# FFN's second product: inner tiles 4 to 15 in two blocks of seven block products instead of eight

## The chip, the core and the metric

The kernel is one program on one core of a Trainium2 chip. The metric is the device time of one execution, in microseconds. TensorE (PE) multiplies; VectorE (DVE) and ScalarE (ACT) prepare operands and take results out of PSUM; GpSimd (POOL) and SyncE (SP) issue DMAs.

## The reference, cut to what matters

One transformer layer on 512 tokens of width 1024, float32 throughout. The change lies in its last third, the feed-forward network:

```python
def _swiglu(h, w_in, w_out):
    g, u = jnp.split(h @ w_in, 2, axis=-1)
    return (jax.nn.silu(g) * u) @ w_out

x = x + g2 * _swiglu(_modulate(x, norm_ffn[l], sh2, sc2), w_ffn_in[l], w_ffn_out[l])
...
return _rmsnorm(x, norm_final)
```

The inner width is 2816, that is 22 tiles of 128. `g2` holds one gate per output channel.

## The kernel before, in words

**Three matmuls for one.** Every float32 operand is held as a high part (a rounding to `fp32r`) and a low part (what the rounding left). ACT makes the high part (`nc.scalar.copy`) and DVE subtracts it from the value to get the low part. `mm3` multiplies high by high, high by low and low by high: lines L187, L188 and L189, three matmuls for each 128-row slice of the inner dimension. `mm3_low_last` (L194, L195, L197) is the same with all matmuls of the weights' low parts at the end.

**Layout.** Channels lie on partitions and tokens on columns. The input of the FFN, `hp`, is held as four quarters (two halves of the channels by two halves of the 512 tokens, `T` = 512, `TC` = 256): `B11`, `B21`, `B22` and so on.

**FFN in.** For each of the 22 inner tiles there is a gate tile and an up tile. Tiles 0 to 2 are multiplied plainly. Tiles 3 to 21 go through `front` and `back`, called a *pair* here: the gate and up weights of tile j as the two rows of a 2 by 2 block matrix, the halves of the input channels as its columns, so that seven block products replace eight (Winograd's form of Strassen's scheme). A pair needs the sums S1 to S4 of weight quarters and the sums N1, N2, T3, T4 of input quarters. The input's sums were made once. The weights' sums and splits are made for each pair by `prepare`:

- loads: the gate tile into `wr` (3 buffers), the up tile into `ur` (2 buffers), both issued by SP;
- `A11`: high part on ACT, low part on DVE (`direct`, L1025 and L1027);
- S1 and S2 on DVE (L1042, L1043), split 1024 wide into `gh`/`gl`; S3 and S4 (L1048, L1049) into `wh`/`wl`;
- `A12` and `A22`: high part on ACT (L1025), its negative of the raw weight's rounding on ACT (L1029), and then a DMA issued by POOL that adds the raw weight from DRAM to it (L1030, accumulating DMA), so that DVE has nothing to do for them.

A product is 4 slices of 3 matmuls, 128x128 weights by 256 columns. I name the products in the order in which they run: `front` has f1 (A11 by B11), f2 (S1 by N1), f3 (S2 by N2), f4 (A12 by B21), `back` has b1 (S3 by T3), b2 (S4 by B22), b3 (A22 by T4). The loop in `strassen` staggers them: while pair j runs its front, pair j-1 runs its back, in the order f1 f2 b1 f3 b2 f4 b3. Between them stand short steps that read and write PSUM: ACT copies (L1068, L1072), DVE additions (L1075, L1086), the gate function on ACT (L1079, L1089), the two products gate times up on DVE (L1090, L1093, the latter after b3), and the split of the finished tile into `act` (L176, L177).

**FFN out.** When a block of inner tiles is done, `ffn_out` multiplies it plainly: for each of the 8 output tiles, 3 matmuls of 512 columns for each inner tile of the block, weights split by `wload` (L157 on ACT, L158 on DVE, two buffers each of `wh`, `wl`), and DVE adds g2 times the result to the residual `x1` in SBUF (L1251). Blocks are tiles 0 to 7, 8 to 14 and 15 to 21. The last block runs in halves of the tokens, with the final norm behind it.

**Order.** In this part the order on each engine is set by a scheduler with costs of its own; PE, ACT and DVE then run their lists strictly in order. DMAs wait in the lists of SP and POOL, in order too.

## Time and profile before

| | |
|---|---|
| median of the runs (lowest, highest) | 885.57 us (885.19, 886.25) |
| time of the profiled execution | 886.11 us |
| its span in the profile | 884.3 us |
| PE busy, share of the span | 874.4 us, 99% |
| DVE, ACT, POOL busy | 614.7, 436.7, 66.7 us |
| matmuls | 5920 recorded (5579 rows in PE's list, repeats merged) |
| granted TensorE clock, mean | 0.998 |

Times in rows of the profile count from the start of the span. A row of a timeline has the start, the duration, the engine, the line and the tiles written and read; in brackets stands the idle time of the engine before it and who ended it. Matmuls and most other instructions overlap with the next of their engine, so what one costs in a row of many is the distance of two starts, not the duration. In a table of groups, the last columns are busy time, mean duration and idle time before.

### The profile page before, as it was taken

How to read it: one execution, taken by the hardware profiler on the slowest of the kernel's cores; microseconds unless marked ns; L12 is line 12 of the kernel's file. 1: busy time of each engine (PE TensorE's matmuls, PEld its weight loads, DVE VectorE, ACT ScalarE, POOL GpSimd, SP SyncE). 2: the span in 40 equal slices, each digit the busy share in tenths (PEclk: the TensorE clock that was granted, in tenths of full speed). 3: DMA queues.
4: the chain of work that ended last, by engine and by line, in shares of the span. 5: the costliest groups of instructions: out<-in, count | busy, mean ns of one | idle time of the engine just before them, and what ended most of it. 6: DMA issues, size and time to landing. Idle time of an engine off the chain costs nothing.

```text
span 884.3 us, 15057 instructions
## 1 busy us (share of the span) xinstructions
PE 874.4 (99%) x5920; PEld 797.7 (90%) x5920; DVE 614.7 (70%) x1187; ACT 436.7 (49%) x823; POOL 66.7 (8%) x93
## 2 busy tenths in 40 slices
PE   9999999999999999999999999999999999999997
PEld 7689798899888998889988899999889998899996
DVE  4678677877876787767886767795366753867644
ACT  4464354455344453444455446673255741666542
POOL 0000010020000100000000000120011100111000
PEclk9999999999999999999999999999999999999999
DMA  9863021436252542434454830384366643755502
GB/s 349 324 196 113 25 72 57 164 113 180 72 187 88 170 141 84 155 109 135 142 149 125 294 111 1 104 221 107 95 176 147 145 119 87 206 142 125 144 1 96
DMA packets 41446, 120.88 MB, mean 137 GB/s; under 512 B 4480, under 2 KB 8864, under 8 KB 40352
## 3 DMA queue, kind: packets, MB, share of 16 engines
q1 hardware_dynamic: 35904, 109.96, 38.2%
q0 software_dynamic: 5472, 9.96, 6.8%
q8 instruction: 46, 0.75, 0.3%
q14 instruction: 24, 0.20, 0.1%
HBM read 116.22 MB, written 3.69 MB: 136 GB/s over the span
## 4 chain that ended last, share of the span: by engine, by line
PE 96%; DVE 1%; ACT 1%; DMA 1%; issue 0%; DVEq 0%; SPq 0%; ACTq 0%
PE ps L187 14%; PE ps L189 13%; PE ps L188 13%; PE ps L197 8%; PE ps L195 8%; PE ps L194 8%; PE pat L347 3%; PE ps L578 3%; PE ps L579 3%; PE ps L580 3%; PE pat L187 2%; PE pat L189 2%; PE pat L188 2%; PE pat L792 2%; PE pat L793 2%; PE pat L794 2%
## 5 line engine op out<-in xcount | busy, mean ns | idle before, releaser
L157 ACT CAST wh<-wr 128x1024 fp32r<-128x1024 f32 (+3 forms) x78 | 78.9, 1011 | 102.7 <-PE ps L188 45.6
L158 DVE TENSOR_TENSOR wl<-wr,wh 128x1024 fp32r<-128x1024 f32 (+3 forms) x78 | 92.6, 1188 | 35.9 <-ACT wh L157 23.8
L194 PE MATMUL ps<-a,wh 128*128 128x512 f32 x272 | 106.5, 392 | 0.0
L195 PE MATMUL ps<-a,wh 128*128 128x512 f32 x272 | 106.3, 391 | 0.0
L187 PE MATMUL ps<-act,wh 128*128 128x512 f32 (+1 forms) x199 | 69.2, 348 | 0.0
L188 PE MATMUL ps<-act,wh 128*128 128x512 f32 (+1 forms) x199 | 69.0, 347 | 0.0
L189 PE MATMUL ps<-act,wl 128*128 128x512 f32 (+1 forms) x199 | 69.0, 347 | 0.0
L197 PE MATMUL ps<-a,wl 128*128 128x512 f32 x272 | 68.0, 390 | 0.0
L195 PEld LDWEIGHTS ps<-a,wh 128*128 128x128 f32 x272 | 51.1, 188 | 10.2
L194 PEld LDWEIGHTS ps<-a,wh 128*128 128x128 f32 x272 | 51.1, 188 | 10.2
L197 PEld LDWEIGHTS ps<-a,wl 128*128 128x128 f32 x272 | 50.8, 188 | 10.5
L1030 POOL DMA_DIRECT2D ol<-in_wffi x38 | 33.4, 897 | 254.7 <-ACT ol L1029 124.4
L187 PE MATMUL ps<-hp,gh 128*128 128x256 f32 x176 | 49.9, 284 | 0.4 <-ACT gh L176 0.4
L189 PE MATMUL ps<-hp,ol 128*128 128x256 f32 x176 | 48.8, 277 | 0.5 <-DVE ol L1027 0.5
L188 PE MATMUL ps<-hp,gh 128*128 128x256 f32 x176 | 49.0, 278 | 0.0
L1251 DVE SCALAR_TENSOR_TENSOR x<-ps,lb,x 128x512 f32<-128x512 f32 (+1 forms) x32 | 19.6, 616 | 42.1 <-PE ps L189 42.1
L189 PE MATMUL ps<-hp,gl 128*128 128x256 f32 x176 | 48.9, 278 | 0.0
L187 PE MATMUL ps<-hp,oh 128*128 128x256 f32 x176 | 48.8, 277 | 0.0
L188 PE MATMUL ps<-hp,oh 128*128 128x256 f32 x176 | 48.7, 277 | 0.0
L537 DVE SCALAR_TENSOR_TENSOR pb<-pb,crow_s 128x1024 f32<-128x1024 f32 x32 | 38.9, 1233 | 10.1 <-DMA pb<-in_wada_b 10.1
L187 PEld LDWEIGHTS ps<-act,wh 128*128 128x128 f32 x199 | 37.5, 188 | 4.8
L188 PEld LDWEIGHTS ps<-act,wh 128*128 128x128 f32 x199 | 37.5, 188 | 4.8
(365 smaller groups left out, 2726.4 us busy)
## 6 DMA issues: line engine op xcount, KB each, us to landing
wr<-in_w SPq DMA_DIRECT2D x42, 512.0 KB, 3.5
pb<-in_wada_b SPq DMA_DIRECT2D x32, 512.0 KB, 4.2
wr<-in_wffi SPq DMA_DIRECT2D x25, 512.0 KB, 4.3
ur<-in_wffi SPq DMA_DIRECT2D x19, 512.0 KB, 4.0
ol<-in_wffi POOLq DMA_DIRECT2D x38, 256.0 KB, 4.9
ada<-in_wada_a SPq DMA_DIRECT2D x8, 1024.0 KB, 9.8
wr<-in_wffo SPq DMA_DIRECT2D x16, 448.0 KB, 3.6
wr<-in_wout SPq DMA_DIRECT2D x8, 512.0 KB, 3.5
```

The costliest lines, as they stand in the source:

```text
L157: nc.scalar.copy(wh, raw[:, :n])
L158: V.tensor_sub(wl, raw[:, :n], wh.bitcast(F32))
L187: nc.tensor.matmul(dst, wh, ah, start=first and i == 0, stop=False, skip_group_check=on)
L188: nc.tensor.matmul(dst, wh, al, start=False, stop=False, skip_group_check=on)
L189: nc.tensor.matmul(dst, wl, ah, start=False, stop=last and i == n - 1, skip_group_check=on)
L194: nc.tensor.matmul(dst, wh, ah, start=first and i == 0, stop=False)
L195: nc.tensor.matmul(dst, wh, al, start=False, stop=False)
L197: nc.tensor.matmul(dst, wl, ah, start=False, stop=last and i == len(wparts) - 1)
L347: nc.tensor.matmul(acc0[i], w_first[k][i][w], aT[k][x], start=k + w + x == 0, stop=k == KT - 1 and w == 1)
L537: V.scalar_tensor_tensor(wa[:, :D], wa[:, :D], 0.5, crow_s, ALU.mult, ALU.mult, accum_out=mods[:, i:i + 1])
L578: nc.tensor.matmul(acc[:, :n], ah, wh, start=kk == 0, stop=False)
L1030: nc.gpsimd.dma_start(l, dram, accum_op=ALU.add)
```

## The change

- Pair 3 now runs its back at once, and the four inner tiles 0 to 3 go through the plain product (`ffn_out`, 12 matmuls of 512 columns for an output tile). The residual `x1` is then stored to a DRAM buffer `x1d`, and its SBUF room is given up.
- Tiles 4 to 9 and 10 to 15 form two blocks. In a block, the even and odd inner tiles are the two halves of the inner dimension: the even tile's two token halves are B11 and B12 of a second 2 by 2 product, the odd tile's are B21 and B22. The classes `Even` and `Odd` are pairs that at their end also make this second product's operand (`Fed`): the parts 11, 21, 22 and the sums N1, T3, N2, T4, split on ACT and DVE into a tile `bo`. In both, `A11` gets its low part by POOL's DMA as well (`sent` has A11, A12, A22).
- After the six pairs of a block come four `Out` items, one for two output tiles each. An `Out` has the same seven products, f1 to b3, with 3 slices in place of 4: 9 matmuls of 256 columns each, 63 in all. Its weights go through the same `prepare`, 384 and 768 wide, strided by 128; A11 and A12 get their low parts on DVE, A22 by DMA. Its results are scaled by g2 (or its negative, `ng2`) on ACT and added to `x1d` by an accumulating DMA of POOL, 256 KB for each output tile.
- `run` chains pairs and Outs in one stagger. Where the first `Out` of a block follows the last `Odd`, the back of the `Odd` runs as a whole, and f1 and f2 of the second `Out` come before f3 of the first (`joint`). I call this place the joint of the block.
- The last block has tiles 16 to 21, six in place of seven; `x1` is loaded back from `x1d` during its pairs.
- `sg`, which holds the weights' sums, becomes two buffers of half the size, so S1/S2 and S3/S4 no longer share one.

```diff
-    open_pool("late2", ("x1", "hp"), "right")
+    open_pool("late2", ("hp",), "right")
     open_pool("late3", ("sg", "ur"), "right")
+    open_pool("late4", ("x1",), "right")
...
         def direct(nm, w, dram):
-            h, l = S("oh", F32R), S("ol", F32R)
-            nc.scalar.copy(h, w)
-            if dram is None:
-                V.tensor_sub(l, w, h.bitcast(F32))
+            h, l = S("oh", F32R)[:, :n], S("ol", F32R)[:, :n]
+            nc.scalar.copy(tiled(h), w)
+            if nm not in sent:
+                V.tensor_sub(tiled(l), w, tiled(h).bitcast(F32))
             else:
-                nc.scalar.activation(l, w, AF.Copy, scale=-1.0)
-                nc.gpsimd.dma_start(l, dram, accum_op=ALU.add)
-            p[nm] = ptiles(h, l)
+                nc.scalar.activation(tiled(l), w, AF.Copy, scale=-1.0)
+                nc.gpsimd.dma_start(tiled(l), dram, accum_op=ALU.add)
+            p[nm] = ptiles(h, l, 0, n)
...
+    class Even(Pair):
+        sent = ("A11", "A12", "A22")
...
+        def done(self):
+            split(self.s[:, :TC], *self.to.one)
+            V.tensor_sub(self.to.n[:, :TC], self.s[:, :TC], self.s[:, TC:])
+            if self.last:
+                self.to.cast(0, 1)
+
+    class Odd(Pair):
+        sent = ("A11", "A12", "A22")
...
+        def second(self, y):
+            super().second(y)
+            s = self.s[:, TC:]
+            V.tensor_sub(self.t3, s, self.even.s[:, TC:])
+            V.scalar_tensor_tensor(self.n2, self.n1, -1.0, s, ALU.mult, ALU.subtract)
+            if self.last:
+                self.to.cast(1, 3)
+
+        def done(self):
+            split(self.s, *self.to.two)
+            V.scalar_tensor_tensor(self.t4, self.n2, -1.0, self.s[:, :TC], ALU.mult, ALU.subtract)
+            self.to.cast(*((3, 4) if self.last else (0, 4)))
+
+    class Out(Pair):
+        sent = ("A22",)
...
+        def third(self, x):
+            self.o1 = S("tmp")
+            V.tensor_add(self.o1[:, TC:], x, self.q[:, :TC])
+            self.scaled(self.o1[:, TC:], self.o1[:, TC:], ng2)
+
+        def second(self, y):
+            self.scaled(self.o[:, TC:], y, g2)
+            nc.gpsimd.dma_start(x1d[2 * self.j], self.o, accum_op=ALU.add)
+
+        def fourth(self, x):
+            self.scaled(self.o1[:, :TC], x, ng2)
+            nc.gpsimd.dma_start(x1d[2 * self.j + 1], self.o1, accum_op=ALU.add)
...
+            joint = isinstance(it, Out) and not isinstance(prev, Out)
+            if not it.begun:
                 next(f)
                 next(f)
-            early = False
+            if joint:
+                for _ in b:
+                    pass
+                after.f = after.front()
+                next(after.f)
+                next(after.f)
+                after.begun = True
...
-    for c0, c1 in ((0, 8), (8, 15)):
-        strassen(max(c0, NP), c1, fr if c0 == 0 else None)
-        turn_[0] = (c1 - 1) % 3
-        for j in range(KT):
-            ffn_out(j, ALL, wchunk(j, c0, c1), c0, c1)
-    c0, c1 = 15, FT
+    for _ in run([third]).back():
+        pass
+    c1 = NP + 1
+    turn_[0] = NP % 3
+    for j in range(KT):
+        ffn_out(j, ALL, wchunk(j, 0, c1), 0, c1)
+        nc.sync.dma_start(x1d[j], x1[j])
+    close_pool("late4")
     close_pool("late0")
-    open_pool("late0", ("act", "before_act"))
...
+    open_pool("late0", ("bo", "nf", "ev"))
+    items, turn = [], itertools.count(NP + 1)
+    for c0 in (4, 10):
+        evens = []
+        for j in range(c0, c0 + 6, 2):
+            evens.append(Even(j, next(turn), j == c0 + 4))
+            items += [evens[-1], Odd(j + 1, next(turn), evens[-1])]
+        items += [Out(j, next(turn), evens, c0, c0 + 6) for j in range(KT // 2)]
+    c0, c1 = 16, FT
+    plain = [Pair(j, next(turn)) for j in range(c0, c1)]
...
+        elif it in plain:
+            for j in itertools.islice(back_, 2):
+                nc.sync.dma_start(x1[j], x1d[j])
```

How the lists of the engines differ, at three places. In these rows a name has its own number and that of its instance; high parts end in `h`, low parts in `l`.

PE before, from the last matmuls of pair 7 (weights `oh_1150`, `ol_1151`) into the first plain product of the first block, whose operands are the eight inner tiles `act`:

```order
L187 MATMUL ps1079_6265<-hp_972_5494,oh_1150_6653 128x256
L188 MATMUL ps1079_6265<-hp_973_5495,oh_1150_6653 128x256
L189 MATMUL ps1079_6265<-hp_972_5494,ol_1151_6654 128x256
L194 MATMUL ps1080_6266<-act_1008_5789,wh_1163_6900 128x512
L195 MATMUL ps1080_6266<-act_1009_5790,wh_1163_6900 128x512
L194 MATMUL ps1080_6266<-act_1020_5811,wh_1163_6900 128x512
L195 MATMUL ps1080_6266<-act_1021_5812,wh_1163_6900 128x512
```

PE now, at the joint of the first block. After the last matmul of b3 of pair 8 stand the six matmuls of f1 of the first Out on `bo_1149` and `bo_1183`; the piece begins with the last of these. `bo_1149`, `bo_1183`, `bo_1217` are the operands made by the three Evens and Odds, `oh_1223`/`ol_1224` A11 of the first Out, `gh_1225`/`gl_1226` its S1, and `wh_1212` S3 of pair 9:

```order
L189 MATMUL ps1081_6273<-bo_1183_6921,ol_1224_7215 128x256
L187 MATMUL ps1083_6275<-bo_1149_6673,gh_1225_7220 128x256
L188 MATMUL ps1083_6275<-bo_1149_6673,gh_1225_7220 128x256
L189 MATMUL ps1083_6275<-bo_1149_6673,gl_1226_7221 128x256
L187 MATMUL ps1081_6273<-bo_1217_7187,oh_1223_7214 128x256
L187 MATMUL ps1083_6275<-bo_1183_6921,gh_1225_7220 128x256
L188 MATMUL ps1083_6275<-bo_1183_6921,gh_1225_7220 128x256
L189 MATMUL ps1083_6275<-bo_1183_6921,gl_1226_7221 128x256
L187 MATMUL ps1080_6272<-hp_972_5497,wh_1212_7097 128x256
L188 MATMUL ps1080_6272<-hp_973_5498,wh_1212_7097 128x256
L188 MATMUL ps1081_6273<-bo_1217_7187,oh_1223_7214 128x256
```

The last operand, `bo_1217`, is read first by the tenth matmul after b3 (its high part) and by the sixteenth (the last row here, which multiplies A11's high part by its low part); before, the tile finished last was read only by the last 3 of 24 matmuls of 512 columns.

ACT before, near the end of the first plain block: the casts of the plain weights of output tiles 2 to 6 and 7 (`wh_1169` to `wh_1181`, `wh_1184`), and between them the weights of pair 8, whose A11 is `oh_1189`:

```order
L157 CAST wh_1178_7055<-wr_1177_7053 128x1024
L157 CAST wh_1181_7086<-wr_1180_7084 128x1024
L1025 CAST oh_1189_7151<-wr_1186_7146 128x512
L176 CAST gh_1191_7157<-sg_1188_7150 128x1024
L1025 CAST oh_1193_7161<-wr_1186_7146 128x512
L1029 ACTIVATE ol_1194_7162<-wr_1186_7146 128x512
```

ACT now, at the same place for pair 4: plain weights of output tiles 5, 6 and 7 are `wh_1112`, `wh_1115`, `wh_1118`; A11 of pair 4 is `oh_1123`/`ol_1124`.

```order
L157 CAST wh_1112_6492<-wr_1111_6490 128x512
L157 CAST wh_1115_6512<-wr_1114_6510 128x512
L1030 CAST oh_1123_6560<-wr_1120_6555 128x512
L157 CAST wh_1118_6532<-wr_1117_6530 128x512
L1034 ACTIVATE ol_1124_6561<-wr_1120_6555 128x512
L176 CAST gh_1125_6567<-sg_1122_6559 128x1024
```

A11's low part now starts on ACT (L1034) and goes on by POOL's DMA, and it stands behind the cast for output tile 7; before, DVE made it from the cast.

ACT now, in the third Out of the first block: results of the second and third Out (L1220), and behind them A11 and A12 of pair 10 (`oh_1289`/`ol_1290`, `oh_1293`). `tmp_1284` is written after b3 of the second Out:

```order
L1220 ACTIVATE tmp_1285_7662<-pat1084_6276,lb_5276 128x256
L1220 ACTIVATE tmp_1284_7629<-ps1082_6274,ng2_5499 128x256
L1030 CAST oh_1289_7680<-wr_1286_7675 128x512
L1034 ACTIVATE ol_1290_7681<-wr_1286_7675 128x512
L1030 CAST oh_1293_7691<-wr_1286_7675 128x512
```

Before, a pair's A11 held a cast alone on ACT, as in this piece, where pair 9 is in its front: `tmp_1230` is its gate value, `act_1228` the finished tile 8, `oh_1234` and `oh_1238` are A11 and A12 of pair 11, and `gh_1236` its S1 and S2:

```order
L1079 ACTIVATE tmp_1230_7374<-pat1083_6269 128x256
L1025 CAST oh_1234_7396<-wr_1231_7391 128x512
L176 CAST act_1228_7320<-tmp_1213_7260 128x512
L1025 CAST oh_1238_7406<-wr_1231_7391 128x512
L176 CAST gh_1236_7402<-sg_1233_7395 128x1024
```

What moved: ACT has one more step for each A11, and at the end of the Outs this step stands behind the results of the Out before.

More of the change, by code (lines that the diff above doesn't have):

```diff
@@ L1052, in prepare @@
         yield
-        direct("A22", a22, wffi[2 * j + 1][:, T:])
+        direct("A22", a22, parted(wb)[1])
         yield
-    def prepared(j):
-        for _ in prepare(j):
-            pass
-        return parts[j]
-    banks = []
-    def front(j, p):
-        n = j % 3
-        x, w, z, y = (banks[i][:, :TC] for i in (n, 3, 4 + j % 2, 6 + j % 2))
-        mm3(x, p["A11"], [kt(B11, k) for k in range(4)])
-        nc.scalar.copy(z, x)
-        yield
-        mm3(w, p["S1"], [kt(N1, k) for k in range(4)])
-        q = S("tmp")
-        nc.scalar.copy(q[:, :TC], w)
-        yield
-        mm3(x, p["S2"], [kt(N2, k) for k in range(4)], first=False, on=True)
-        V.tensor_add(y, x, q[:, :TC])
-        yield
-        mm3(z, p["A12"], [kt(B21, k) for k in range(4)], first=False, on=True)
-        s = S("tmp")
-        nc.scalar.activation(s[:, :TC], z, AF.Silu)
-        yield p, x, y, q, s
@@ new lines, in layer_kernel, with __init__, cast @@
+    class Fed:
+        def __init__(self):
+            t = tl("bo", [P, NEXT + 14 * TC], F32R, 3, LINE)[:, NEXT:]
+            h, l = t[:, :7 * TC], t[:, 7 * TC:]
+            self.parts = {nm: (h[:, e * TC:(e + 1) * TC], l[:, e * TC:(e + 1) * TC])
+                          for e, nm in enumerate(("11", "21", "22", "N1", "T3", "N2", "T4"))}
+            self.one, self.two, self.sums = ((h[:, a * TC:b * TC], l[:, a * TC:b * TC]) for a, b in ((0, 1), (1, 3), (3, 7)))
+            self.value = tl("ev", [P, T], F32, 1, LINE)
+            self.n = tl("nf", [P, D], F32, 1, LINE)
+        def cast(self, a, b):
+            split(self.n[:, a * TC:b * TC], *(t[:, a * TC:b * TC] for t in self.sums))
@@ L1211, in layer_kernel @@
         f.low()
-        p = prepare(NP)
+        third = Pair(NP, NP)
+        p = third.prepare()
         next(p)
```

205 lines of the change are left out of this document (150 added, 55 removed).

## Prediction

> **What bounds the kernel now.** I read the page first. Its engine rows and its chain of waits say who sets the end.
>
> ```profile
> span 884.3 us, 15057 instructions
> PE 874.4 (99%) x5920; PEld 797.7 (90%) x5920; DVE 614.7 (70%) x1187; ACT 436.7 (49%) x823; POOL 66.7 (8%) x93
> PE 96%; DVE 1%; ACT 1%; DMA 1%; issue 0%; DVEq 0%; SPq 0%; ACTq 0%
> ```
>
> TensorE is busy for 99% of the span and carries 96% of the chain. Matmuls overlap, so busy time alone proves little; I therefore asked for stretches of the FFN. The first is the first plain FFN-out product (192 matmuls of 512 columns, a few records more by overlap at its ends), the third is four whole pairs (336 matmuls of 256); the second and fourth are the first three products after each plain block, 36 matmuls each.
>
> ```profile
> core 0: us, PE busy (x) PEld busy (x) DVE busy (x) ACT busy (x) POOL busy (x), PEclk, DMA share, GB/s
> 617.33:660.87 43.54, 43.54 (x195) 36.05 (x193) 22.90 (x29) 14.28 (x19) 2.62 (x3) 1.00 0.46 127
> 660.87:665.33 4.46, 4.46 (x38) 4.27 (x36) 4.43 (x6) 2.85 (x5) 0.87 (x1) 1.00 0.58 142
> 680.44:719.12 38.68, 38.68 (x339) 38.68 (x337) 27.20 (x45) 24.06 (x45) 6.95 (x8) 1.00 0.67 159
> 766.84:771.33 4.49, 4.49 (x37) 4.30 (x36) 4.46 (x7) 3.29 (x6) 0.87 (x1) 1.00 0.57 146
> ```
>
> A 512-column matmul costs 43.54 / 192 = 0.2268 us, a 256-column one in the pairs 38.68 / 336 = 0.1151 us, at full granted clock (1.00). TensorE has no hole in either stage, while DVE is busy for 70% and ACT for 62% of the pairs. So the number of matmul columns sets the time as long as operands come in time. Where they did not, in the FFN, the timeline of PE around the start of pair 4 shows:
>
> ```profile
> 570.86 0.28 PE L188 MATMUL pat<-hp,oh 128*128 128x256 f32 x1
> 571.53 0.39 PE L189 MATMUL pat<-hp,ol 128*128 128x256 f32 x1 [0.39 <-DMA ol<-in_wffi]
> ...
> 572.94 0.28 PE L188 MATMUL ps<-hp,oh 128*128 128x256 f32 x1
> 573.71 0.38 PE L189 MATMUL ps<-hp,ol 128*128 128x256 f32 x1 [0.49 <-DVE ol L1027]
> 573.93 0.28 PE L187 MATMUL ps<-hp,oh 128*128 128x256 f32 x1
> ...
> 574.85 0.28 PE L189 MATMUL ps<-hp,ol 128*128 128x256 f32 x1
> 575.50 0.38 PE L187 MATMUL ps<-hp,gh 128*128 128x256 f32 x1 [0.37 <-ACT gh L176]
> 575.72 0.28 PE L188 MATMUL ps<-hp,gh 128*128 128x256 f32 x1
> ```
>
> The first wait is A12 of pair 3; the second and third are A11 and S1 of pair 4, whose weights were not ready.
>
> **The change, part by part.** *Matmuls.* Tiles 4 to 15 leave the plain product: 12 x 8 x 3 = 288 matmuls of 512 columns, 288 x 0.2268 = 65.3 us. Eight Outs of 63 matmuls of 256 columns come: 504 x 0.1151 = 58.0 us. That is **-7.3**. At half a 512-column step, 0.1134 us, it would be -8.2; at the 4.49 / 36 = 0.1247 of the last row, which holds short waits as well, -2.5. Other matmuls stay: 10 plain inner tiles and 19 pairs.
>
> A rule speaks against this step. The Trainium skill, TensorE: Matmul & The Clock Gate, section Back-to-back issue gap, says that the sustained distance of matmuls with a weight load each falls only from about 131 ns at 512 columns to about 81 ns at 128, so that halving columns does not halve time. Here the two rows above give 0.1151 to 0.2268, a ratio of 0.51; the trace does not agree with it.
>
> *Holes that go.* Pair 4 now starts after a plain product of eight output tiles, not right behind pair 3, so the waits at 573.71 and 575.50 go: (573.71 - 572.94) + (573.93 - 573.71) + (575.50 - 574.85) + (575.72 - 575.50) less four steps of 0.115 = **-1.4**. What is late next is A22 of pair 3, since its back now runs at once: its DMA is issued at 572.21 and takes 4.9 us in the middle, to 577.1, while PE gets there about two plain matmuls and two products later than the end of A12's product (572.8), at 572.8 + 0.45 + 26 x 0.1151 = 576.3. I take **+0.5**, between 0 and the longest landing's 4.8.
>
> ```profile
> 572.21 0.88 POOL L1030 DMA_DIRECT2D ol<-in_wffi  x1 [3.95 <-ACT ol L1029]
> DMA to landing us min/median/max: 3.6/4.9/8.9
> wr<-in_wffi SPq DMA_DIRECT2D x25, 512.0 KB, 4.3
> yd<-tmp SPq DMA_DIRECT2D x6, 256.0 KB, 2.9
> tmp<-yd SPq DMA_DIRECT2D x6, 256.0 KB, 3.9
> ```
>
> The two starts after plain blocks cost 4.46 and 4.49 for 36 matmuls in place of 4.14; these starts are gone, since Outs and pairs run in one stagger: **-0.65**.
>
> *Start of pair 4.* A plain output tile now takes 12 x 0.2268 = 2.72 us instead of 5.4, and A11's low part goes through POOL. The steps come from the first plain product, whose first output tile ends with a matmul at 622.56:
>
> ```profile
> 622.56 0.39 PE L189 MATMUL ps<-act,wl 128*128 128x512 f32 x1
> 622.81 1.05 ACT L157 CAST wh<-wr 128x1024 fp32r<-128x1024 f32 x1 [3.07 <-PE ps L188]
> 622.99 0.75 DVE L1251 SCALAR_TENSOR_TENSOR x<-ps,lb,x 128x512 f32<-128x512 f32 x1 [2.52 <-PE ps L189]
> 623.89 1.23 DVE L158 TENSOR_TENSOR wl<-wr,wh 128x1024 fp32r<-128x1024 f32 x1
> ```
>
> Counted from the start of output tile 4: the split that frees the third `wr` buffer ends at about 1.8 (0.25 to the cast, 0.62 of it, then DVE's result and a half-width low part), the load lands 4.3 later, at 6.1. ACT then does A11's high part, the cast for output tile 7 and A11's negative, 0.53 + 0.53 + 0.63, to 7.8; POOL's DMA lands 4.9 after its issue, at 12.8. PE needs it with the third matmul after four output tiles, at 10.9 + 0.2. The wait is **+1.7**; with landings from 3.6 to 8.9 it is 0.4 to 5.7. Behind the load on SP stands a store of `x1`, 256 KB, and behind ACT's A11 the cast for output tile 7: this cast starts at 6.6 where PE needs it, with DVE's low part, at 8.2, so it is covered by half a microsecond.
>
> By the Trainium skill, DMA: Bandwidth & Descriptors, section Anatomy of one DMA, a DMA of this kind takes 2.0 us and its bytes at 436 GB/s, 2.6 us for 256 KB, and this wait would be nothing. The landing row has 3.6 as its least, so the trace does not agree, and I keep 4.9.
>
> *The two joints.* Before, the tile finished last was covered by 21 matmuls of 512 columns. Now TensorE wants the last Even's operand with the tenth matmul behind its b3, 10 x 0.1151 = 1.15 us behind the last matmul's start. The steps, from the end of a pair and from the steady pairs:
>
> ```profile
> 613.05 0.28 PE L189 MATMUL ps<-hp,ol 128*128 128x256 f32 x1
> 613.37 0.43 DVE L1093 SCALAR_TENSOR_TENSOR tmp<-ps,tmp 128x256 f32<-128x256 f32 x1 [0.19 <-PE ps L189]
> 613.83 0.62 ACT L176 CAST act<-tmp 128x512 fp32r<-128x512 f32 x1 [1.44 <-DVE tmp L1093]
> ...
> 680.02 0.36 ACT L1068 COPY pat<-ps 128x256 f32<-128x256 f32 x1
> ...
> 684.45 1.23 DVE L177 TENSOR_TENSOR wl<-sg,wh 128x1024 fp32r<-128x1024 f32 x1 [1.83 <-ACT wh L176]
> 685.60 0.42 DVE L1090 SCALAR_TENSOR_TENSOR tmp<-tmp,tmp 128x256 f32<-128x256 f32 x1
> 685.93 0.68 DVE L1042 TENSOR_TENSOR sg<-ur 128x512 f32<-128x512 f32 x1
> 686.54 0.42 DVE L1093 SCALAR_TENSOR_TENSOR tmp<-ps,tmp 128x256 f32<-128x256 f32 x1
> ```
>
> The product starts 0.32 behind the last matmul, its cast 0.78, and with 0.37 for 256 columns the high part is there at 1.15: just in time if DVE is free. But by the steps of DVE in a row (684.45 to 685.60 is 1.15 us for 1024 columns, then 0.33 for 256 and 0.61 for 512, and between them 0.47 for 384 and 0.87 for 768) DVE is then still at S3 and S4 of the second Out and about 0.3 late; the sum N1 and two low parts follow, and the low part of N1 comes 0.2 later than PE wants it: 0.5 in all. In the joint's second half DVE does, behind the last Odd's product, T3, N2, a weight's low part, T4 and two low parts of 512 columns, 4 x 0.33 + 0.47 + 2 x 0.61 = 3.0, and starts about 1.0 late behind the wide low part of S3 and S4; PE has 32 matmuls, 3.7, as cover, so 0.4 remain, and 0.3 for the two short waits of PE on DVE's reads of PSUM behind it. Together 1.2, twice: **+2.4**. The ends are 0.1 each (DVE free) and 2.5 each (DVE behind by both wide low parts).
>
> *The Outs between.* An Out takes PE 63 x 0.1151 = 7.25 us. DVE does six steps of 384, two of 768, two of 256: 2.82 + 1.74 + 0.66 = 5.2. ACT does four of 384, two of 768 and six of 256: about 5. Both fit, so I cost it at nothing; the cover is the 2 us that are left.
>
> *Pair 10's A11* stands on ACT behind the second Out's last result: 0.32 + 0.30 + 0.53 + 0.63 + 4.9 = 6.7 behind b3, and PE needs it 7.25 + 0.23 behind. Two accumulating DMAs to DRAM, which the trace does not have, are in flight before it; a store (2.9) and a load (3.9) bound each at 6.8 from above, 2.9 from below. I take **+0.4**; the ends are 0 and, with a landing of 8.9, 3.2. In the other pairs A11's chain has a whole pair (9.67) as cover.
>
> *The residual* is stored during the plain product and loaded during the last pairs, off every path; two of the loads wait for the last Out's accumulation, some 40 us before use.
>
> **Sum:** -7.3 - 1.4 + 0.5 - 0.65 + 1.7 + 2.4 + 0.4 = -4.35. The profiled execution took 886.11 (span 884.3 and 1.8 around it), 0.5 above the median of 885.57, so the forecast stands at 885.57 - 4.35 = 881.2, rounded to 881.3.
>
> **Rivals.** *All new waits are covered* (the scheduler's spread of matmuls at the joint, shorter landings): -7.3 - 1.4 - 0.65, so 876.2. For it: PE waits on nothing inside the steady pairs. Against: the computed landings. *DVE becomes the bound of the Outs*, the way it ends slower: at 684.45 DVE sits 1.83 us until ACT has cast S3/S4, because the `wh` buffer comes free only with b2. If that wait and 0.4 of others stay as long in an Out, DVE needs 5.2 + 2.2 = 7.4 for 7.25 of PE, and in the second Out, which has five products left (5.2 us), 2.3 too much: 8 x 0.2 + 2 x 2.4 = 6.4, which makes 887.6. It decides from the point where an Out loses 0.55 us. Against: with less work behind b2 the wait grows only where there is time for it. *Accumulations to DRAM hold the result buffers*: there are seven `tmp`, so one comes back to ACT about 9.4 us after its DMA's issue; with landings of 10.4 us, the copy behind f2 would be 1 us late in three items of each block, +6, so 887.2. The longest row, 8.9, speaks against. *Weight loads set the pace*: weight loads are busy for all 38.68 of the pairs' 38.68 us, and with nine matmuls on a weight row they might hold TensorE. At 75% of a 512-column step, 504 x 0.170 = 85.7, +20 on the plain product's 65.3 and 909. The pairs' own 0.1151 speaks against it; this is the skill's issue gap rule from above, taken at 256 columns between its two figures.
>
> **Chances.** Forecast 0.55, all covered 0.20, DVE as bound 0.13, buffers held 0.10, weight loads 0.02. A measurement can tell about 0.2% (1.8 us) from no change. Faster than 883.8: the first two but for 0.05, and 0.02 of the slower rivals, 0.72. Slower than 887.3: 0.14, half and more of the last three. The rest, 0.14, lies between. The range leaves out the best half of "all covered" and the worst of the slower ones: 876.0 to 886.5.
>
> **What would show it.** Right: the Outs' 504 matmuls at 0.113 to 0.118; PE waiting on a DMA at pair 4's first product, and on ACT and DVE in f1 to f3 of the first Out of each block; no hole at 571 to 576 but that of A12 and perhaps A22. Wrong: holes in PE in every Out with DVE's rows unbroken; ACT waiting for POOL's DMAs before a copy of f2; or a matmul step above 0.12 in the Outs.

## The result, and the profile after

| | before | after |
|---|---|---|
| median of the runs (lowest, highest) | 885.68 us (885.19, 886.25) | 915.73 us (911.85, 917.67) |
| ratio, with its 95% interval | | 1.0334 (1.0299 to 1.0368) |
| span of the profiled execution | 884.3 us | 915.9 us |

The forecast was 881.3 us with a range of 876.0 to 886.5. The change made the kernel 30 us slower. The page of after has these lines; the last three are groups of DMA issues, with the count, the size of each and the median time from issue to landing.

```profile
span 915.9 us, 15854 instructions
PE 878.8 (96%) x6112; PEld 809.6 (88%) x6112; DVE 645.7 (70%) x1274; ACT 479.1 (52%) x933; POOL 100.9 (11%) x129
...
PE 77%; issue 8%; DMA 7%; DVE 4%; ACT 3%; POOL 1%; DVEq 0%; SPq 0%; POOLq 0%; ACTq 0%
...
wr<-in_wffi SPq DMA_DIRECT2D x25, 512.0 KB, 5.3
ol<-in_wffi POOLq DMA_DIRECT2D x50, 256.0 KB, 6.3
...
x1d<-tmp POOLq DMA_DIRECT2D x16, 256.0 KB, 8.4
```

TensorE carried 96% of the chain of waits before and carries 77% now; DMAs stand in it with 7%. Another 8% is "issue", time in which the profile shows nothing that the engine waited for. The landings that the prediction took from before (4.3 for `wr`, 4.9 for the low parts) are all longer. DVE is as busy as it was (70%), but an average over stages can't say whether DVE was the bound in the Outs; a run further down does. This profile is of the slowest execution, and single waits differ between executions: in the run "late loads, a miss", whose program is the same up to 800 us, the two longest waits for a low part are 2.00 and 4.90 us where this one has 4.41 and 6.96. So the size of one hole is good to some 2 us, and a difference of two medians in which 915.73 stands to some 3. The waits of PE by whom it waited for (total, times, longest):

```profile
PE ps L189 <- DMA ol<-in_wffi: 15.1, 4, 7.0
PE ps L187 <- ACT pat L1085: 6.3, 7, 2.1
PE ps L187 <- DVE tmp L1123: 5.7, 2, 5.3
```

The stretches of the FFN say when: the start of pair 4, a stretch of Outs in which PE waits for nothing, the end of the first Outs, four pairs of the second block, the end of the second Outs, and the first of the last pairs; the three rows at the end are parts of these.

```profile
core 0: us, PE busy (x) PEld busy (x) DVE busy (x) ACT busy (x) POOL busy (x), PEclk, DMA share, GB/s
598.00:618.00 20.00, 15.59 (x99) 14.80 (x98) 12.51 (x19) 13.18 (x24) 6.98 (x8) 0.83 0.99 257
676.96:685.12 8.16, 8.16 (x75) 8.16 (x74) 5.82 (x11) 5.39 (x12) 3.16 (x3) 1.00 0.69 162
690.00:707.00 17.00, 7.90 (x58) 7.50 (x57) 8.15 (x12) 9.40 (x19) 8.47 (x9) 0.79 1.01 206
723.88:764.70 40.82, 39.28 (x339) 38.88 (x338) 33.02 (x58) 29.43 (x55) 8.60 (x10) 1.00 0.77 172
792.00:810.00 18.00, 15.93 (x137) 15.53 (x136) 12.16 (x19) 13.12 (x27) 7.58 (x8) 1.00 0.99 216
810.00:839.00 29.00, 22.54 (x168) 21.93 (x167) 16.75 (x27) 14.73 (x29) 6.08 (x7) 0.90 0.78 211
815.00:822.00 7.00, 7.00 (x61) 7.00 (x61) 5.67 (x10) 4.10 (x7) 0.87 (x1) 1.00 1.04 244
822.00:833.00 11.00, 6.10 (x50) 5.69 (x48) 2.73 (x6) 2.25 (x5) 0.86 (x1) 1.00 0.90 288
723.88:735.00 11.12, 9.87 (x86) 9.68 (x85) 8.45 (x14) 8.15 (x16) 2.58 (x3) 1.00 1.03 237
```

At the start of pair 4 and at the end of the first and of the second Outs (the first, third and fifth row), where PE loses time, the column of the DMA share reads 0.99 to 1.01: the 16 DMA engines are full. The fourth row is a mean of 0.77, but its first 11 us, the last row, read 1.03. In the last pairs the two do not fall together: at 815 to 822 the share is 1.04 and PE is busy for all of the 7 us, and PE loses its time behind it, at 822 to 833. In the second row, a stretch of Outs, 72 matmuls (three more records overlap the ends) take 8.16 us, 0.1133 each. So the saving in matmuls is there, 288 x 0.2268 - 504 x 0.1133 = 8.2 us, a little more than forecast. The largest holes, in the timeline of PE at the start of pair 4:

```profile
601.50 0.28 PE L188 MATMUL ps<-hp,oh 128*128 128x256 f32 x1
606.19 0.58 PE L189 MATMUL ps<-hp,ol 128*128 128x256 f32 x1 [4.41 <-DMA ol<-in_wffi]
606.57 0.41 PE L187 MATMUL ps<-hp,oh 128*128 128x256 f32 x1
606.78 0.41 PE L188 MATMUL ps<-hp,oh 128*128 128x256 f32 x1
```

PE waits 4.41 us for A11's low part, and then a matmul takes 0.21 us instead of 0.113 (from 606.57 to 606.78): the mean granted clock of this stretch is 0.83. By the distances of starts, f1 and f2 of pair 4 take 7.11 and 2.56 in place of 1.36 each, 7.0 us lost. At pair 10 the same reads:

```profile
690.96 0.62 ACT L1030 CAST oh<-wr 128x512 fp32r<-128x512 f32 x1
692.40 2.80 POOL L1035 DMA_DIRECT2D ol<-in_wffi  x2
693.47 0.39 PE L187 MATMUL ps<-bo,gh 128*128 128x256 f32 x1 [2.15 <-ACT pat L1085]
704.80 0.58 PE L189 MATMUL ps<-hp,ol 128*128 128x256 f32 x1 [6.96 <-DMA ol<-in_wffi]
```

The first DMA of the second row is issued at 692.40 and has landed at 704.8, after 12.4 us. The wait at 693.47 is of another kind: ACT, which works through its list in order, is busy without a break from 687.36, with casts of weights, A22, the Out's results and then A11 and A12 of pair 10, and the copy of f1 that PE needs stands behind them. The same 2.15 stands in both runs on late loads of the residual. The losses are 2.3 us at 691 and 9.5 at 697. The third place is SP's list in the first of the last pairs:

```profile
811.35 3.23 SPq L1453 DMA_DIRECT2D x<-x1d  x6
814.69 0.41 SPq L1018 DMA_DIRECT2D wr<-in_wffi  x1
815.76 5.68 SPq L1453 DMA_DIRECT2D x<-x1d  x2
821.54 0.39 SPq L1017 DMA_DIRECT2D ur<-in_wffi  x1
```

The eight loads of the residual go out as soon as the last Outs are read, the last two wait for the last accumulation, and the `ur` load of pair 20 stands behind them and lands at 832.0, 10.4 us after its issue. DVE, which has the sums of these weights ahead of an addition that PE needs in pair 17, waits with it, and PE for DVE: the 5.3 us of the table of waits; with the next product, whose matmuls run at half speed, 8.1 us are lost. The expectations below call this place pair 19. A22 of pair 3 takes 4.09 instead of 1.36 us, 2.7 lost.

### The profile page after: what moved, and what is told of

It is laid out like the page before. It is cut to its first block, busy times and chain, and to the rows that moved or that the text cites. A ratio compares the mean times of both kernels' runs of the same rounds, so it can differ in the third digit from the quotient of the medians.

```text
span 915.9 us, 15854 instructions
## 1 busy us (share of the span) xinstructions
PE 878.8 (96%) x6112; PEld 809.6 (88%) x6112; DVE 645.7 (70%) x1274; ACT 479.1 (52%) x933; POOL 100.9 (11%) x129
## 4 chain that ended last, share of the span: by engine, by line
PE 77%; issue 8%; DMA 7%; DVE 4%; ACT 3%; POOL 1%; DVEq 0%; SPq 0%; POOLq 0%; ACTq 0%
PE ps L187 9%; PE ps L188 9%; PE ps L189 9%; PE ps L197 8%; PE ps L195 8%; PE ps L194 8%; DMA ol<-in_wffi 3%; PE pat L347 3%; PE ps L579 3%; PE ps L578 3%; PE ps L580 3%; DMA ur<-in_wffi 2%; PE pat L792 2%; PE pat L793 2%; PE pat L794 2%
## 5 line engine op out<-in xcount | busy, mean ns | idle before, releaser
L157 ACT CAST wh<-wr 128x1024 fp32r<-128x1024 f32 (+3 forms) x70 | 67.4, 963 | 64.4 <-PE ps L195 34.8
L158 DVE TENSOR_TENSOR wl<-wr,wh 128x1024 fp32r<-128x1024 f32 (+3 forms) x70 | 79.2, 1131 | 29.6 <-ACT wh L157 18.3
L1035 POOL DMA_DIRECT2D ol<-in_wffi x50 | 45.8, 934 | 183.8 <-ACT ol L1034 99.5
L189 PE MATMUL ps<-hp,ol 128*128 128x256 f32 x176 | 51.5, 293 | 15.1 <-DMA ol<-in_wffi 15.1
L195 PEld LDWEIGHTS ps<-a,wh 128*128 128x128 f32 x272 | 51.1, 188 | 10.2
L194 PEld LDWEIGHTS ps<-a,wh 128*128 128x128 f32 x272 | 51.1, 188 | 10.2
L187 PE MATMUL ps<-hp,oh 128*128 128x256 f32 x176 | 51.1, 290 | 5.7 <-DVE tmp L1123 5.7
L188 PE MATMUL ps<-hp,oh 128*128 128x256 f32 x176 | 50.7, 288 | 0.0
L176 ACT CAST gh<-sg 128x1024 fp32r<-128x1024 f32 (+1 forms) x27 | 26.7, 988 | 44.2 <-DVE sg L1049 32.4
L189 PEld LDWEIGHTS ps<-hp,ol 128*128 128x128 f32 x176 | 35.3, 201 | 15.8 <-DMA ol<-in_wffi 15.8
L537 DVE SCALAR_TENSOR_TENSOR pb<-pb,crow_s 128x1024 f32<-128x1024 f32 x32 | 38.9, 1233 | 10.2 <-DMA pb<-in_wada_b 10.2
L177 DVE TENSOR_TENSOR gl<-sg,gh 128x1024 fp32r<-128x1024 f32 (+1 forms) x27 | 30.9, 1145 | 21.1 <-ACT gh L176 21.1
L1048 DVE TENSOR_TENSOR sg<-ur 128x512 f32<-128x512 f32 (+1 forms) x27 | 17.5, 648 | 37.8 <-DMA ur<-in_wffi 35.7
L792 PE MATMUL pat<-vh,Sp 128*128 128x258 f32 x144 | 41.0, 285 | 0.0
L793 PE MATMUL pat<-vl,Sp 128*128 128x258 f32 x144 | 40.6, 282 | 0.0
## 6 DMA issues: line engine op xcount, KB each, us to landing
ada<-in_wada_a SPq DMA_DIRECT2D x8, 1024.0 KB, 10.1
```

Source lines behind the costliest of these rows:

```text
L157: nc.scalar.copy(wh, raw[:, :n])
L158: V.tensor_sub(wl, raw[:, :n], wh.bitcast(F32))
L187: nc.tensor.matmul(dst, wh, ah, start=first and i == 0, stop=False, skip_group_check=on)
L188: nc.tensor.matmul(dst, wh, al, start=False, stop=False, skip_group_check=on)
L189: nc.tensor.matmul(dst, wl, ah, start=False, stop=last and i == n - 1, skip_group_check=on)
L194: nc.tensor.matmul(dst, wh, ah, start=first and i == 0, stop=False)
```

## The experiments

**Theories.** A: the change adds so many DMAs that the 16 engines are full in bursts; landings stretch from 5 to between 8 and 13 us, and PE waits. B: nothing is full; A11's chain through ACT, ACT, POOL and DMA is too long by itself where a block starts. C: POOL's queue serves its DMAs one after the other, so A11 stands behind the results. The runs lay on several chips; each ratio is to before in the same run on its own chip, where it took 885.5 to 886.2. An expectation that names a theory gives what that theory would make of the run.

**A11 on DVE in all Evens and Odds: 905.66 us**

```diff
-        sent = ("A11", "A12", "A22")
+        sent = ("A12", "A22")
```

> A11 of the Evens and Odds gets its low part on DVE again, as before the change (12 accumulating DMAs of 256 KB less); all else as changed. Theory A (the 16 DMA engines are full: shares of 0.99 and 1.01 at 598 to 618 and 690 to 707 us, and landings stretch to 8 to 13 us): the share in the pairs falls from about 0.8 to 0.65, A11's waits go and those on A12, A22 and the weight loads shrink; the Outs' results still fill the engines, so 3 to 5 us of the 12 at pair 10 stay: about 900 us (895 to 904). Theory B (nothing is full; the chain ACT, ACT, POOL, DMA of A11 is too long for the two starts): exactly A11's two waits go with the slow matmuls behind them, 6.9 + 9.5, and all the other waits stay as they are: about 899, with landings of the other DMAs unchanged. Theory C (POOL's queue serves its DMAs one after the other): as A for the DMAs of POOL, but the loads issued by SP land as late as now.

It is 10.1 faster than the change (ratio to before 1.0230, 1.0194 to 1.0266). The waits of PE in the FFN now:

```profile
PE ps L187 <- ACT pat L1085: 8.8, 10, 2.0
PE ps L187 <- DVE tmp L1123: 6.1, 3, 5.4
PE ps L189 <- DMA ol<-in_wffi: 1.2, 1, 1.2
```

A11's waits are gone, and the waits for ACT have grown from 6.3 to 8.8. Both theories expected a faster kernel, 895 to 904 and about 899, so the size misses both, and the run does not tell them apart. A11's DMAs were not all of it: the share at the end of the first Outs is still 0.98 (684 to 710).

**Results left out: 903.04 us (one run)**

```diff
-            nc.gpsimd.dma_start(x1d[2 * self.j], self.o, accum_op=ALU.add)
...
-            nc.gpsimd.dma_start(x1d[2 * self.j + 1], self.o1, accum_op=ALU.add)
```

> Leaves out the 16 accumulating DMAs of the Outs' results to the DRAM residual, so the second product of tiles 4 to 15 doesn't reach the output; everything else runs. Theory A: the holes that follow the Outs go nearly whole (2.3 at 691, 9.5 at 697, 1.5 at 724, 1.9 at 792, some 1 around 811), those at pair 4 (6.9) and at pair 19 (8) stay: about 900 us (897 to 904), with loads of SP landing in 4 to 5 us at 690 to 707 instead of 7 to 9. Theory B: A11's chain of pair 10 stays as long, so the wait at 697 stays within 2 us of 8: 911 to 915. Theory C: as A for POOL's DMAs, but the loads issued by SP don't land earlier.

The kernel leaves out what the second product of these tiles adds to the output. Every step of DVE and ACT stays, only DMAs are gone. This is 12.7 less, within A's range (897 to 904) and below B's (911 to 915). At 684 to 707, around the start of pair 10, the stretch reads, and below it the landings of `ol` and of `wr` there:

```profile
684.00:707.00 23.00, 19.62 (x153) 19.23 (x152) 13.79 (x19) 17.79 (x33) 5.60 (x6) 0.93 0.74 165
```

```profile
DMA to landing us min/median/max: 5.2/6.0/7.9
DMA to landing us min/median/max: 5.1/6.0/7.0
```

In the changed kernel the same landings were, for `ol` and for the one `wr` issued at 690 to 707:

```profile
DMA to landing us min/median/max: 4.7/10.7/12.9
DMA to landing us min/median/max: 9.4/9.4/9.4
```

Taking DMAs out of POOL's queue shortens the loads of SP's queue as well, 9.4 (a single load) to about 6.0: C falls as the whole cause; that order in POOL's queue adds something to A11's landing is not excluded. B said that A11's wait stays; f1 and f2 of pair 10 lose 4.1 now instead of 9.5, so B alone falls too. By the Trainium skill, DMA: Bandwidth & Descriptors, section Queues, rings and completion order, every one of the 16 engines takes turns between the queues that have work for it; these rows agree with that.

**Late loads of the residual, a miss: 914.04 us**

```diff
-        elif it in plain:
+        elif it in plain[2:]:
```

> The eight loads of the residual back to SBUF go with the items from the third of the last six pairs on, two each, instead of from the second; nothing is left out. Theory A: six loads no longer go out at 811 together with two weight loads and three accumulations, and the wait of 5.5 + 2.5 at pair 19's A12 and the next A11 goes: 907 us (905 to 910). Rival (the wait at 827 comes from DVE's order, not from late loads: the row names DVE): no change, 914 to 917.

The edit did not do what it says. The loads depend on nothing that is late, and the scheduler put them where they had been, so the run is nearly the changed kernel once more:

```profile
809.57 2.18 SPq L1453 DMA_DIRECT2D x<-x1d  x4
...
812.44 7.16 SPq L1453 DMA_DIRECT2D x<-x1d  x4
819.69 0.38 SPq L1017 DMA_DIRECT2D ur<-in_wffi  x1
```

**Before, with A11 through DMA: 892.77 us**

```diff
-        direct("A11", a11)
+        direct("A11", a11, wffi[2 * j][:, :T] if 4 <= j < 15 else None)
```

> The kernel before, with one part of the change alone: A11 of pairs 4 to 14 gets its low part by POOL's accumulating DMA (11 DMAs of 256 KB more). Theory A: the DMA share of the steady pairs goes from 0.67 to about 0.83 and median landings from 4.9 to about 6, PE still waits for nothing there; at the start of pair 4, where the share was 0.92 already, 3 to 6 us more are lost, at the start of pair 8 up to 1: 889 to 893 us. Theory B: A11's chain of about 7 us is on the path at each start of a block: 2 to 4 at pair 4, 1 to 3 at pair 8, independent of the share: 889 to 892. What tells them apart is the landing at pair 4 (A: 7 and more; B: 5).

1.0075 (1.0059 to 1.0090), 6.6 us, all of it at pair 4, where the row of A11's first low part is the first below. The second is four steady pairs:

```profile
579.48 0.58 PE L189 MATMUL ps<-hp,ol 128*128 128x256 f32 x1 [4.14 <-DMA ol<-in_wffi]
```

```profile
686.20:724.90 38.70, 38.70 (x337) 38.70 (x336) 24.60 (x41) 24.84 (x47) 9.30 (x11) 1.00 0.81 184
```

In the pairs the share rose from 0.67 to 0.81, 1.35 us of the engines for each accumulation of 256 KB (0.14 x 9.67), and PE does not wait. At pair 8, behind a plain product of 43 us, the first two products lose 0.3 as in before: A11's chain is covered there. That speaks against B as a cost at every start. The expectation had named the landing at pair 4 as what tells the two apart (7 and more by A, 5 by B): the DMA was issued at 572.61 and landed after 6.8 us, nearer to A.

**Two ways of loading before without touching its chains.** The first, 16 copies between DRAM buffers, gave 885.64 us and tells nothing: they had nothing to wait for and went out at 49 to 86 us.

> The kernel before, with 16 copies of 512 KB from a weight in DRAM to an unused DRAM buffer, issued by SP, four in each of pairs 9 to 12; nothing else changes, POOL's queue has no DMA more, and no engine computes anything more. Theory A (the 16 DMA engines are shared, and PE waits when they are full): the share in pairs 9 to 12 goes from 0.67 to 1.0, POOL's accumulating DMAs land after 8 to 12 us instead of 5, and PE waits there: 10 to 16 us in all, 895 to 903. Theory B (fixed chain) and theory C (order inside POOL's queue): POOL's DMAs land after 5 us as before, PE waits at most for weight loads that stand behind the copies on SP: 886 to 890.

```profile
L1109 SPq DMA_DIRECT2D dd<-in_wffi x16: 488/540/598, 48.8 to 85.6; - x16
```

The second stores finished tiles to DRAM, plainly and without accumulating, and did load the pairs:

```diff
+            if 10 <= j < 14:
+                for e in range(6):
+                    nc.sync.dma_start(dd[6 * (j - 10) + e], act[j - 2][e % 2].bitcast(F32))
```

> The run with copies again, with a load that can't go out early: the kernel before, with 24 stores of 256 KB from finished act tiles to an unused DRAM buffer, issued by SP, six in each of pairs 10 to 13 (the tile stored is that of two pairs earlier). Six stores are about 5 us of the 16 engines for a pair of 9.67 us. Theory A (full engines): the share in pairs 10 to 13 goes from 0.67 to nearly 1.0, POOL's DMAs land after 8 us and more instead of 4.9, and PE waits: 889 to 896 us. Theories B and C (fixed chain, order in POOL's queue, to which nothing is added): landings of POOL's DMAs stay at 5, 885 to 887.

Measured: 885.78 us, ratio 0.9995 (0.9986 to 1.0005). The four pairs, and the landings of `ol` in them:

```profile
680.44:719.12 38.68, 38.68 (x339) 38.68 (x338) 26.99 (x45) 23.82 (x44) 6.52 (x8) 1.00 1.04 318
```

```profile
DMA to landing us min/median/max: 6.1/6.5/7.5
```

The share was 1.04, as A wanted it, the landings went from a median of 4.5 in these pairs to 6.5, and PE waited for nothing. (The six stores took 3.6 us of the engines for a pair, 0.37 x 9.67, not about 5 as I had expected.) So full engines alone cost nothing: **A as I had put it falls as well.** What is left is both halves together. How much is in flight seems to set how late a DMA lands; the lead of the operand, the time from the issue until PE needs it, sets whether that is paid. In steady pairs a lead of over 7.5 us is there. The share alone does not give the landing: at 1.04 it is 6.5 here, and in the changed kernel, at 0.99 to 1.01, 8 to 12. That more was issued there than the engines could do is the likely reason; no run here counts it.

**The two first edits together: 895.0 us (one run)**

> The first two edits together: A11's low part on DVE, and the accumulating DMAs of the Outs' results left out (the second product of tiles 4 to 15 doesn't reach the output). Theory A: both unload the same engines at the same places, so they overlap: against the changed kernel's 915.7, less 10.1 and 12.7 would be 893; what stays is mostly pair 19's wait of 5.7 behind the residual's loads and the joints: 891 to 895. If the two were separate causes that add up to more, below 890.

20.7 less than the change, against 10.1 and 12.7 singly; so they overlap by 2.1, no more than the spread of these runs. The time lies at the upper end of what was expected. Like the second edit, the kernel leaves out the second product of tiles 4 to 15.

**No DMA of the residual: 900.42 us; the same with A11 on DVE: 890.09 us.** In the code, the stores of `x1`, the results' DMAs and the loads go, and POOL sets the residual to zero, so the residual and the second product of tiles 4 to 15 are missing from the output.

```diff
-        nc.sync.dma_start(x1d[j], x1[j])
...
-                nc.sync.dma_start(x1[j], x1d[j])
+                nc.gpsimd.memset(x1[j], 0.0)
```

> No DMA of the residual at all: neither its stores, nor the accumulations of the Outs' results, nor its loads (POOL sets it to zero instead), so residual and second product of tiles 4 to 15 are left out; A11 goes through DMA as in the change. Theory A: pair 4 (6.9 in the change) falls to 2 to 4, pair 10 to 3, pair 19's wait (8.1) goes: 893 us (890 to 897). Theory B: A11's waits at pair 4 and 10 stay at 5 to 8 each: 898 to 903.

> No DMA of the residual (as in the run before it, the same parts left out) and A11's low part on DVE: the change with its matmuls, its joints and its order, but with a DMA load like that of before. Theory A: what is left are the matmuls saved (8.2 at the 0.1133 us of the Outs), two joints of 1.3 each, and A22 of pair 3 with 1.5: 882.5 us (880 to 884.5), faster than before. Rival (DVE, with 0.85 of its time busy in the Evens and Odds, or the joints, hold PE as well): 887 or more.

Both are slower than A expected; the first lies in B's range (898 to 903), the second in the rival's (887 or more). In the first, f1 and f2 of pairs 4 and 5 lose 11 us without any store of the residual: the loads and accumulations of pairs 4 to 7, which all start there, fill the engines nearly by themselves:

```profile
596.00:615.00 19.00, 12.36 (x61) 11.22 (x60) 11.42 (x15) 10.88 (x19) 5.24 (x6) 0.78 0.89 230
```

A11's low parts of pairs 4 and 5 land after 6.9 and 10.1 us there. Pair 10 loses about 3.5, not the 5 to 8 by which B would have come to its range, so the total alone does not make B right. In the second run 4.6 us against before remained (1.0048, 1.0033 to 1.0063), so something else cost, too; two runs below give 3.2 to the opening and 5.9 to A22 of the Outs.

**A11 on DVE in pairs 4, 5, 10 and 11 alone: 905.51 us**

```diff
+            if j in (4, 10):
+                self.sent = ("A12", "A22")
...
+            if j in (5, 11):
+                self.sent = ("A12", "A22")
```

> As the changed kernel, with A11's low part on DVE in pairs 4, 5, 10 and 11 alone, the first two of each block (4 accumulating DMAs less instead of 12). If A11's DMA costs only where a block starts, since there the engines are full and nothing covers the chain, this gives all of what the edit in all 12 pairs gave: 904 to 907 us against 905.7. If the steady pairs pay for it too (theory A without the places), only a third: 911 to 913.

Four DMAs fewer give all that twelve gave (10.2 and 10.1 us). For A11 the place decides, not the amount.

**Late loads, forced: 909.94 us**

```diff
-        elif it in plain:
+        elif it in plain[2:]:
             for j in itertools.islice(back_, 2):
+                nc.gpsimd.tensor_copy(x1[j][:, :1], act[it.j - 1][0][:, :1].bitcast(F32))
                 nc.sync.dma_start(x1[j], x1d[j])
```

> The late loads of the residual once more, now forced: before each load POOL copies one column of the act tile finished last into the tile to be loaded, so that the load can't go out before the third of the last six pairs has run. Nothing is left out. Theory A: the eight loads no longer share the engines with the last accumulations and the loads of pairs 18 to 20; the wait of 5.5 + 2.5 at pair 19 goes, 907 to 909. If the last Outs' own results and the pairs' loads fill the engines there by themselves: 2 to 4 us only, 911 to 914.

POOL's copy writes a column of the tile that the load fills, and reads a tile that is finished late, so the load has to wait for it. SP now has the weights of the last pairs ahead of the loads:

```profile
816.43 0.33 SPq L1017 DMA_DIRECT2D ur<-in_wffi  x1
819.53 0.33 SPq L154 DMA_DIRECT2D wr<-in_wffo  x1
825.47 0.33 SPq L1017 DMA_DIRECT2D ur<-in_wffi  x1
828.04 0.93 SPq L1454 DMA_DIRECT2D x<-x1d  x2
```

The wait of 5.3 us for DVE is gone, and 5.8 us of the median; some 2 come back as short waits in the last pairs.

**A22 of the Outs on DVE alone: 908.89 us**

```diff
-        sent = ("A22",)
+        sent = ()
```

> The changed kernel with A22 of the Outs on DVE (8 accumulating DMAs of 192 KB less), nothing else. The waits at b3 of the second and third Out and the A11 of pair 10, which stands behind these DMAs: 3 to 6 us less, 910 to 913 us. If DVE has no room in an Out: 916 and more.

6.8 less, a little more than expected. Eight DMAs of 192 KB are gone, four in each block of Outs, but with each of them goes a step of ACT (0.52 us) as well. In the profiles PE's waits for low parts fall from 15.1 to 10.1 us and those for ACT from 6.3 to 3.5, and the 2.15 at 693 to 0.31. Between two kernels without any DMA of the residual, where the share at 684 to 710 is only 0.75 to 0.79, the same edit gives 5.9 (890.09 and, below, 884.15). So this cost is not shown to be the DMA engines' time; between that and ACT's list it stays open.

**The three edits together: 894.11 us**

> The best version that the runs point to, complete in what it computes: A11 on DVE in all Evens and Odds, A22 of the Outs on DVE as well (8 accumulating DMAs of 192 KB less), and the late loads of the residual. Theory A: 905.7 less about 8 for pair 19, less 2 to 4 for the Outs: 893 to 896, still slower than before, since the results' 16 accumulations stay. Rival (DVE now has too much in the Outs: 5.2 + 0.5 of 7.25 us): 898 or more.

10.1 + 5.8 + 6.8 = 22.7 singly, 21.6 together. The stretch around the start of pair 10, with the landings of its `ol`:

```profile
684.00:710.00 26.00, 25.75 (x219) 25.32 (x218) 17.95 (x26) 17.91 (x36) 8.65 (x10) 1.00 0.98 225
```

```profile
DMA to landing us min/median/max: 5.4/7.0/8.7
```

The engines are still full (0.98), and PE is busy for 25.75 of 26 us, with eight matmuls (0.9 us) fewer than the kernel without any DMA of the residual, below, at the same place. That is the second time that a full stretch costs next to nothing once no DMA with a short lead is in it. It is the best version of the change that computes all, and it is slower than before (1.0088, 1.0069 to 1.0107).

**The opening: block sizes alone in before, 888.71 us; the same with A11 through DMA, 894.45 us**

```diff
-    for c0, c1 in ((0, 8), (8, 15)):
+    for c0, c1 in ((0, 4), (4, 10), (10, 16)):
...
-    c0, c1 = 15, FT
+    c0, c1 = 16, FT
```

> The kernel before with the change's block sizes alone: blocks of 4, 6, 6 and 6 inner tiles, all multiplied plainly, pair 3 back at once; no Outs, no new DMAs, as many matmuls as before. What the opening costs: the waits at 571 to 576 go (1.4), pair 3's A22 waits instead (0.5 by the sum, 1 to 2.7 in the traces of the changed kernel), one more start after a plain block (0.35), A11 of pair 4 stays on DVE: 886 to 888 us. If the short plain product by itself leaves the weights of pair 4 late (the burst of loads at 0.9 and more of the engines): 889 and more.

> The same with A11 of pairs 4 to 15 by POOL's accumulating DMA: no residual DMAs, no Outs. With the steady landing of 4.9 us (the sum on record) pair 4 waits 1.7 and pair 10, behind a plain block of six tiles with 4.1 us for an output tile, nothing: 2 us over the run before it. If the burst stretches the landings and the waits put the matmuls to 0.213 us each, as at 601 to 611 of the changed kernel: 6 to 11 us over the run before it, nearly all at pairs 4 and 5.

The opening alone costs 3.2 us (1.0039, 1.0026 to 1.0052), somewhat more than expected; A22 of pair 3 loses 1.5 in its profile. A11's DMA behind it costs 5.7 more, without Outs and without any DMA of the residual, just under the 6 to 11 expected of a full stretch and well over the 2 of the chain alone. In that run its DMA is issued at 595.52; the rows of PE:

```profile
599.50 0.28 PE L188 MATMUL ps<-hp,oh 128*128 128x256 f32 x1
602.74 0.58 PE L189 MATMUL ps<-hp,ol 128*128 128x256 f32 x1 [2.96 <-DMA ol<-in_wffi]
```

The landing took 7.2. At before's 4.9 the wait would have been 0.8 of the 2.96, so here, too, the greater part is the stretched landing and the smaller the chain; the slow matmuls behind it make the loss at pair 4 4.7 us.

**Without any DMA of the residual, A11 and A22 on DVE: 884.15 us**

> The lightest form: no DMA of the residual (left out as before: its stores, its loads, the accumulations of the Outs' results, so the output lacks the second product of tiles 4 to 15), A11 of Evens and Odds and A22 of the Outs on DVE. If DMAs are all that the change loses, this comes to its matmuls and joints: 882 to 885 us. If the steps of DVE and ACT in the Evens, Odds and joints cost by themselves: 887 to 890, no faster than before.

The ratio is 0.9986 (0.9975 to 0.9997): hardly to be told from before, in a kernel that leaves out the residual and the second product of tiles 4 to 15. The first joint and the three Outs behind it:

```profile
656.00:663.08 7.08, 6.49 (x57) 6.29 (x55) 5.42 (x13) 3.53 (x8) 0.00 (x0) 1.00 0.39 108
663.08:687.02 23.94, 23.93 (x209) 23.67 (x208) 22.37 (x42) 17.88 (x38) 0.87 (x1) 1.00 0.48 139
```

54 matmuls in 7.08 and 207 in 23.94 are 0.96 and 0.49 over 0.1133 each: a joint costs 1.45. With DVE busy for 22.37 of 23.94 us the Outs, the joint's second half with them, still take 0.1157 for each matmul (23.94 / 207). So DVE is not the bound of the Outs.

**The three edits, results left out: 887.50 us**

> The complete kernel with the three edits (A11 and the Outs' A22 on DVE, late loads of the residual; 894.1) without the accumulations of the Outs' results (their second product doesn't reach the output); the residual is still stored and loaded. Between 894.1 and the 884.2 without any DMA of the residual: if the results' accumulations are what is left, 885 to 888; if the stores and loads of the residual are, 891 to 894.

It lies in the first of the two expected ranges (1.0029, 1.0016 to 1.0043): of the last 10 us the results' accumulations are 6.6 and the residual's plain stores and loads 3.4. The kernel leaves out the second product of tiles 4 to 15.

**The account.** From 915.7, each step as a difference of medians: A11 and Outs' A22 on DVE and late loads -21.6 (894.1), results' accumulations -6.6 (887.5), stores and loads -3.4 (884.15). From there to before's 885.5: the matmuls -8.2, the opening +3.2, two joints +2.9, which makes 883.4; the 0.8 that is left is within the spread. The starts that the prediction had at -0.65 are not in this sum, and no run takes short waits in Evens and Odds apart.

## Why the prediction was wrong

- *Matmuls, -7.3:* right, -8.2 measured. The rival of weight loads is refuted by 0.1133, and with it, in this shape, the Trainium skill's rule on the issue gap that the prediction named.
- *Joints, +2.4:* right in mechanism and size, 2 x 1.45.
- *Holes that go, -1.4 and -0.65:* the two holes at 573 and 575 are gone, as forecast, and others took their place. The -0.65 for starts behind plain blocks no run takes apart.
- *A22 of pair 3, +0.5:* the mechanism was right, the size was not: the working itself gives 577.1 - 576.3 = 0.8, of which 0.5 was taken, and 2.7 were lost in the changed kernel, 1.5 with the block sizes alone.
- *Start of pair 4, +1.7:* the place and the chain were right (issue worked out 7.8 behind the start of output tile 4, measured 7.3), the landing was not: 8.1 us, where "POOL's DMA lands 4.9 after its issue" stood. That makes the wait 4.4. The other 2.6 are matmuls at half speed after it, which no term had.
- *Pair 10's A11, +0.4:* this step failed most, 9.5, with 2.3 at ACT before it, which no term had either. I bounded two accumulations in flight by a store and a load, and A11's own landing by 8.9; it took 12.4. Its issue was later, too, 4.8 behind b3 where 1.8 was worked out, because of ACT's list; with a landing of 4.9 it would still have been there at 697.3, before PE needed it at 697.7. The rows came from a stage in which the engines had a third of their time free.
- *The Outs, nothing:* PE does go through them at the pace of the matmuls, but they are not free. The 2 us of cover were free time of DVE and ACT, and their DMAs were not priced: the results' accumulations cost 6.6 to 12.7, 5.4 of the 12.7 at f1 and f2 of pair 10 behind them (4.1 lost there instead of 9.5). A22 of the Outs through ACT and DMA cost 6.8 more; whether by the DMA engines or by ACT's list is open.
- *The residual, "off every path":* failed. It was off the path as an operand, but not as a user of the engines and of SP's list: 5.8 for where its loads stood, 3.4 for its plain stores and loads once they stood late.
- *Rivals:* none held this. DVE as the bound is refuted by the run in which DVE is busy for 93% of the Outs and PE keeps its pace; in the changed kernel no copy behind f2 waited for a result buffer.

One failing is under most of these: I took landings as constants. The row that could have told was quoted, the share of 0.67 in the steady pairs, and I read only the columns of PE, DVE and ACT from it. The DMA column says that 6.5 of 9.67 us were used by two loads of 512 KB and two accumulations; a third accumulation in each pair, and three in each Out (A22 and two results), had to be added to it, and the places where they pile up found.

## What to carry to other kernels

Add up the DMA engines' time for each stage as one adds up an engine's: where a change brings it near the whole, landings from a quieter stage no longer hold. Here they grew 1.4 to 2.5 times (6.5 us for 4.5, 8.1 and 12.4 for 4.9). Then ask for each operand how long its lead is. With a lead longer than the stretched landing a full stretch costs nothing (1.04 of share, no wait). Where a block started here there was no such lead, so keep DMAs out of such a chain. A transfer that nobody waits for still takes its share, and an in-order list can put it ahead of one that is waited for. Add a hole's price behind the wait, too: the matmuls after a wait of 3 us or more ran at half speed here.

## What the runs showed of the hardware

By estimate from the shares, an accumulating DMA of 256 KB takes 1.35 us of the 16 engines (0.67 to 0.81 of 9.67 us), more than twice a plain store: 24 stores of 256 KB raised the share over 38.68 us by 0.37, 0.6 us each. After waits of PE of 2.96 to 6.96 us its matmuls ran at 0.21 us for 3.2 to 5.3 us, and after the 2.15 at 693 they did not. By the Trainium skill, TensorE: Matmul & The Clock Gate, Part 1 on the clock gate, the clock is halved after an idle window of about 3.4 us and comes back after about as long a time of work. The rows agree in the ratio (0.1133 to 0.213) and roughly in the length, 3.2 to 5.3 us of slow matmuls; a wait of 2.96 was enough here.
